# Third product of the attention scores on 64 rows, its two components on different row halves, blocks of scores made in pairs

## The chip, the cores and the metric

The kernel runs on one core of one Trainium2 chip. The metric is the time of one execution on the device, in microseconds. A core has five engines, each with its own queue of instructions that run in order: TensorE (PE; its weight loads are shown apart as PEld), VectorE (DVE), ScalarE (ACT), GpSimd (POOL) and SyncE (SP), which here issues nearly all DMA transfers. Engines wait for each other through semaphores. TensorE multiplies a stationary operand (loaded by a weight load) with a stream of columns, and adds the product up in PSUM.

## What is computed

One decoder layer, x of 2048 tokens by 1024, all in float32: a projection, then two groups of heads side by side (differential attention with 4 heads, and mLSTM with 4 heads), an output projection, and an MLP with squared ReLU. The part that matters is attention. Each head has two components of 64 dimensions, each with its own queries and keys, and one value of 128:

```
s = einsum('bhcqd,bhckd->bhcqk', qb, kb) * scale      # c: 2 components, d: 64
s = where(mask, s, -inf);  p = softmax(s)             # causal
p_diff = p[:, :, 0] - lam * p[:, :, 1]
out = einsum('bhqk,bhkv->bhqv', p_diff, v)            # v: 128
```

## The kernel before

Float32 products are made from two parts. A float32 number x is split into hi (rounded to the type float32r, which TensorE takes in one pass) and lo, the rest. x times y is then hi*hi + hi*lo + lo*hi, three passes (`mm3`, L91 to L95). Some products (transposes, the values of attention, mLSTM) are left in plain float32, of which one product of values or mLSTM shows as two passes in a trace and a transpose as one.

`phase_in` (L189 on) makes the projections, and writes keys and queries of attention, turned and split, to the DRAM tensors Kd and Qd: `Kd[g][h, 0]` is hi and `[h, 1]` is lo, each 128 rows, of which rows 0 to 63 are component 0 and 64 to 127 component 1. `phase_mix` (L503 on) is attention and mLSTM. Its attention goes in 64 units (4 heads h, 16 blocks qb of 128 queries):

- `load_kv` (L528), once in four units: a K tile of 512 keys, [128, 2, 512]. On rows 0 to 63 lies hi and on rows 64 to 127 lo, for component c in `[:, c]`. It takes two DMAs; the values V one.
- `load_q` (L539), once in two units: a Q tile [128, 2, 2, 256]. Both row halves hold the same, hi in `[:, 0]` and lo in `[:, 1]`, per component. Four DMAs.
- `scores` (L549): for each component c and each block j of up to 512 keys two products over all 128 rows into one PSUM tile s (pool psS, three buffers). The first, with Q hi against K hi and lo at once, gives hi*hi + hi*lo; the second, with Q lo, gives lo*hi + lo*lo (L571 to L574). VectorE moves the block from PSUM to the tile p and takes its maximum (L577; the last block with the causal mask, L580). When a component's blocks are done, ScalarE takes exp (L586). After both, p = p0 + cf * p1 is made on VectorE (L596) and, for long rows, in part on ScalarE and GpSimd (L594, L595).
- `values` (L639 on): p is turned by TensorE in 128x128 blocks into tp (L651), copied to pT by ScalarE (L653), and multiplied with V into pv (L656). VectorE writes o (L658).

`ahead` (L614) holds up to four units scored before their values are made. Between the units run the stages of 16 chunks of mLSTM: `chunk_load` (L690; loads E from Md and wb from Wd, each broadcast over rows; GpSimd adds a mask at L705 and ScalarE takes exp at L707), `chunk_scores` (L711; L725 multiplies over 64 rows, the two heads of a pair on different halves), `chunk_values` (L731; L742 over 128 rows and L743 over 64 rows alternate; L749 has 64 columns of the stationary operand) and `chunk_norm`.

The order on each engine is not the order of the code. A scheduler with a timeline of its own sets it when the program is built; each engine then runs its row as it stands.

Of the kernel before, what the change touches and what calls it, by code (L numbers as in the profile page):

```python
# [11 lines left out]
F32 = mybir.dt.float32  # L12
F32R = mybir.dt.float32r
I32 = mybir.dt.int32
AF = mybir.ActivationFunctionType
ALU = mybir.AluOpType
# [486 lines left out]
def phase_mix(tc, a, sc, ident, late):  # L503
    nc = tc.nc
    with ExitStack() as ctx:
        def pool(name, bufs, **kw):
            return ctx.enter_context(tc.tile_pool(name=name, bufs=bufs, reuse_waits="tile", **kw))

        kp = pool("kp", 5, side="right")
        qp = pool("qp", 3, side="right")  # L510
# [3 lines left out]
        psS = pool("psS", 3, space=PSUM)  # L514
        psV = pool("psV", 1, space=PSUM)

        maskq = ce.tile([128, 512], F32, name="maskq")
# [3 lines left out]
        Ks, Vs, Qs, outs = {}, {}, {}, {}  # L521
        n_p = [0]

        def p_tile():
            n_p[0] += 1
            return (pb if n_p[0] % 6 == 0 else pa).tile([128, S], F32, name="p")

        def load_kv(h, g):  # L528
            t = kp.tile([128, 2, 512], F32R, name="K")
            for hl in range(2):  # L530
                nc.sync.dma_start(t[hl * 64:(hl + 1) * 64].bitcast(F32),
                                  sc["Kd"][g][h, hl].rearrange("(c p) t -> p c t", c=2))
            Ks[h, g] = t
            t = kp.tile([128, 4, 128], F32, name="V")
            nc.sync.dma_start(t, sc["Vd"][g][:, h * 128:(h + 1) * 128].rearrange(
                "(b p) v -> p b v", p=128))
            Vs[h, g] = t

        def load_q(h, g):  # L539
            Q = qp.tile([128, 2, 2, 256], F32R, name="Q")  # L540
            o = g % 2 * 256
            for hf in range(2):
                for var in range(2):
                    nc.sync.dma_start(
                        Q[hf * 64:(hf + 1) * 64, var].bitcast(F32),
                        sc["Qd"][g // 2][h, var, :, o:o + 256].rearrange("(c p) t -> p c t", c=2))
            Qs[h, g] = Q

        def scores(u):  # L549
            h, qb = units[u]  # L550
            if qb % 4 == 0:
                load_kv(h, qb // 4)
            if qb % 2 == 0:
                load_q(h, qb // 2)
            Q = Qs[h, qb // 2]
            W = (qb + 1) * 128
            n = qb // 4 + 1
            qo = (qb % 2) * 128
            mx = st.tile([128, 2, 4], F32, name="mx")
            nm = st.tile([128, 2], F32, name="nm")  # L560
            Z = st.tile([128, 2], F32, name="Z")
            if n <= 2:
                t = p_tile()
                p = [t[:, 0:1024], t[:, 1024:2048]]
            else:
                p = [p_tile(), p_tile()]
            for c in range(2):
                pc = p[c]
                for j in range(n):
                    w = min(512, W - j * 512)  # L570
                    ps = psS.tile([128, 512], F32, name="s")  # L571
                    for var in range(2):
                        nc.tensor.matmul(ps[:, :w], Q[:, var, c, qo:qo + 128], Ks[h, j][:, c, 0:w],  # L573
                                         start=(var == 0), stop=(var == 1))  # L574
                    dst = pc[:, j * 512:j * 512 + w]
                    if j < n - 1:
                        nc.vector.tensor_scalar(dst, ps[:, :w], 0.0, None, op0=ALU.add, op1=ALU.max,  # L577
                                                accum_out=mx[:, c, j:j + 1])
                    else:
                        nc.vector.tensor_tensor_reduce(dst, ps[:, :w], maskq[:, 512 - w:512], 1.0, -3.0e38,  # L580
                                                       ALU.add, ALU.max, mx[:, c, j:j + 1])
                if n == 1:
                    nc.vector.tensor_scalar(nm[:, c:c + 1], mx[:, c, 0:1], -1.0, None, op0=ALU.mult)
                else:
                    nc.vector.tensor_reduce(nm[:, c:c + 1], mx[:, c, :n], axis=AX.X, op=ALU.max, negate=True)  # L585
                nc.scalar.activation(pc[:, :W], pc[:, :W], AF.Exp, bias=nm[:, c:c + 1],  # L586
                                     accum_out=Z[:, c:c + 1])
            rz = st.tile([128, 2], F32, name="rz")
            nc.vector.reciprocal(rz, Z)
            cf = st.tile([128, 1], F32, name="cf")  # L590
            nc.vector.scalar_tensor_tensor(cf, Z[:, 0:1], nlam, rz[:, 1:2], op0=ALU.mult, op1=ALU.mult)
            cut = W if W < 1024 else W - int(W * PSH) // 128 * 128
            if cut < W:
                nc.scalar.activation(p[1][:, cut:W], p[1][:, cut:W], AF.Copy, scale=cf)  # L594
                nc.gpsimd.tensor_tensor(p[0][:, cut:W], p[1][:, cut:W], p[0][:, cut:W], op=ALU.add)  # L595
            nc.vector.scalar_tensor_tensor(p[0][:, :cut], p[1][:, :cut], cf, p[0][:, :cut],  # L596
                                           op0=ALU.mult, op1=ALU.add)
            return p[0], rz
# [15 lines left out]
        def ahead(u):  # L614
            held = sum(1 if units[v][1] < 8 else 2 for v in pend)
            while len(pend) < 4:
                v = u + len(pend)
                if v >= len(units):
                    break
                held += 1 if units[v][1] < 8 else 2  # L620
                if held > 7:
                    break
                pend[v] = scores(v)

        pend[0] = scores(0)
        pend[1] = scores(1)
        yield
        raw, w_out = late["raw"], late["w_out"]
# [704 lines left out]
```

## Time and profile before

| | us |
|---|---|
| median of 3 runs (2558.26 to 2561.15) | 2559.36 |
| the profiled execution's own time | 2563.28 |
| its span, first to last instruction | 2561.4 |
| of it 0 to 553.5: projections | 553.5 |
| 553.5 to 1073: attention and mLSTM | 519.5 |
| 1073 to 1281: output projection | 208.0 |
| 1281 to the end: MLP | 1280.4 |

Times in the rows are of one execution. Matmuls are pipelined: the busy time of one includes its way through the array, so a product's own share is read from the distance between starts, not from its length. The granted clock is given as a share of full speed: 1.00 is 2.4 GHz, 0.50 is 1.2 GHz.

### The profile page before, as it was taken

The page shows a single profiled execution, that of the slowest core. Times are in us where ns is not written, and L with a number is a line of the kernel's source. Part 1 is how long each engine was busy: PE and PEld are TensorE (multiplying, and loading weights), DVE is VectorE, ACT ScalarE, POOL GpSimd, SP SyncE. Part 2 cuts the span into 40 slices and gives each one's busy share as a digit, 9 for nine tenths or more (in the row PEclk, how much of TensorE's full clock was granted, in tenths as well). Part 3 has the DMA queues.
Part 4 walks back from the last instruction along what each step waited for, and adds up shares of the span by engine and source line. Part 5 has one row for each costly group of instructions (what it writes and reads, how often), then busy time and mean ns, then how long its engine had stood idle before and what let it go on. Part 6 is the DMA issues. An engine that isn't in the chain of part 4 may idle for free.

```text
span 2561.4 us, 34625 instructions
## 1 busy us (share of the span) xinstructions
PE 2425.0 (95%) x12030; PEld 2040.0 (80%) x12030; DVE 1456.0 (57%) x3132; ACT 1065.2 (42%) x2103; POOL 440.1 (17%) x724
## 2 busy tenths in 40 slices
PE   8999999989879799999939999999999999999998
PEld 6888889987668687888828888888888888887886
DVE  4483441016657588576647667666665543333885
ACT  7210112326656577644524344444444332332433
POOL 0002222104635354432300000000000000000423
PEclk9999999998889899999969999999999999999999
DMA  9323432257653634255774345844358664444784
GB/s 320 130 78 91 125 109 85 55 133 167 145 115 75 148 88 113 83 177 181 236 266 164 136 157 174 350 161 168 133 176 305 222 221 169 146 143 167 282 288 144
DMA packets 296751, 424.35 MB, mean 166 GB/s; under 512 B 23584, under 2 KB 170416, under 8 KB 295040
## 3 DMA queue, kind: packets, MB, share of 16 engines
q1 hardware_dynamic: 296224, 421.94, 51.5%
q8 instruction: 95, 1.56, 0.3%
q14 instruction: 80, 0.66, 0.1%
q0 software_dynamic: 352, 0.20, 0.1%
HBM read 283.56 MB, written 138.49 MB: 165 GB/s over the span
## 4 chain that ended last, share of the span: by engine, by line
PE 76%; DMA 11%; DVE 6%; POOL 2%; ACT 2%; issue 2%; SPq 0%; POOLq 0%; DVEq 0%; ACTq 0%
PE pd L969 16%; PE A L969 14%; PE B L969 10%; PE pp L93 7%; PE pp L94 7%; PE pp L95 7%; DMA br<-in_w_down_dram 3%; PE pv L656 3%; PE s L573 3%; PE po L93 2%; DMA E<-Md 2%; PE po L94 2%; PE po L95 2%; PE tp L651 2%; DMA wb<-Wd 1%
## 5 line engine op out<-in xcount | busy, mean ns | idle before, releaser
L969 PE MATMUL pd<-bo,ao 128*128 128x512 f32 x2688 | 613.8, 390 | 8.3 <-DVE y L1153 4.8
L969 PEld LDWEIGHTS pd<-bo,ao 128*128 128x128 f32 x2688 | 506.2, 188 | 115.8 <-issue 5.2
L969 PE MATMUL A<-B,w 128*128 128x512 f32 x1536 | 359.3, 389 | 0.0
L969 PEld LDWEIGHTS A<-B,w 128*128 128x128 f32 x1536 | 288.3, 188 | 59.7
L969 PE MATMUL B<-B,w 128*128 128x512 f32 x1152 | 274.4, 392 | 19.2 <-ACT w L1059 19.2
L93 PE MATMUL pp<-w,xT 128*128 128x512 f32 (+1 forms) x768 | 271.3, 358 | 9.3 <-ACT w L230 7.8
L94 PE MATMUL pp<-w,xT 128*128 128x512 f32 (+1 forms) x768 | 273.2, 356 | 0.0
L95 PE MATMUL pp<-w,xT 128*128 128x512 f32 (+1 forms) x768 | 271.1, 355 | 0.0
L969 PEld LDWEIGHTS B<-B,w 128*128 128x128 f32 x1152 | 217.9, 189 | 65.0 <-ACT w L1059 19.7
L1211 POOL TENSOR_TENSOR y<-y,g 128x512 f32<-128x512 f32 x32 | 49.2, 1560 | 1183.6 <-ACT jk L1205 1120.2
L1178 ACT CAST ao<-ar 128x1024 fp32r<-128x1024 f32 x112 | 117.8, 1052 | 287.5 <-PE pd L969 150.5
L1153 DVE TENSOR_TENSOR ao<-ar,ao 128x1024 fp32r<-128x1024 f32 x112 | 139.3, 1243 | 152.3 <-ACT ao L1178 152.2
L1026 DVE TENSOR_TENSOR w<-wr,w 128x512 fp32r<-128x512 f32 x224 | 154.0, 689 | 105.0 <-ACT w L1059 103.9
L573 PE MATMUL s<-K,Q 128*128 128x512 f32 (+3 forms) x640 | 193.9, 418 | 13.6 <-DVE p L577 6.6
L1059 ACT CAST w<-wr 128x512 fp32r<-128x512 f32 x224 | 138.8, 621 | 130.6 <-PE B L969 116.8
L656 PE MATMUL pv<-V,pT 128*128 128x128 f32 x1088 | 158.2, 290 | 31.5 <-ACT pT L653 22.9
L656 PEld LDWEIGHTS pv<-V,pT 128*128 128x128 f32 x1088 | 147.4, 202 | 44.0 <-ACT pT L653 26.2
L586 ACT ACTIVATE p<-p,nm 128x128 f32<-128x128 f32 (+15 forms) x128 | 153.5, 1200 | 33.2 <-DVE nm L585 22.1
L93 PEld LDWEIGHTS pp<-w,xT 128*128 128x128 f32 x768 | 144.4, 188 | 25.9 <-ACT w L230 8.7
L577 DVE TENSOR_SCALAR_CACHE_REDUCE p<-s 128x512 f32<-128x512 f32 x192 | 129.0, 684 | 51.6 <-PE s L573 28.4
L94 PEld LDWEIGHTS pp<-w,xT 128*128 128x128 f32 x768 | 144.5, 188 | 15.2 <-DVE w L231 0.3
L95 PEld LDWEIGHTS pp<-w,xT 128*128 128x128 f32 x768 | 144.3, 188 | 15.1
(249 smaller groups left out, 3566.0 us busy)
## 6 DMA issues: line engine op xcount, KB each, us to landing
ud<-u SPq DMA_DIRECT2D x224, 256.0 KB, 2.8
ar<-ud SPq DMA_DIRECT2D x112, 512.0 KB, 4.1
br<-in_w_down_dram SPq DMA_DIRECT2D x224, 256.0 KB, 4.0
wr<-in_w_up_dram SPq DMA_DIRECT2D x128, 256.0 KB, 3.6
Bd<-hl SPq DMA_DIRECT2D x40, 512.0 KB, 3.9
B<-Bd SPq DMA_DIRECT2D x10, 2048.0 KB, 13.8
Q<-Qd SPq DMA_DIRECT2D x128, 128.0 KB, 4.7
raw<-in_xT_dram SPq DMA_DIRECT2D x32, 256.0 KB, 5.0
```

What stands on the lines that cost most here:

```text
L93: nc.tensor.matmul(ps, lhs[0], rhs[0], start=first, stop=False)
L94: nc.tensor.matmul(ps, lhs[0], rhs[1], start=False, stop=False)
L95: nc.tensor.matmul(ps, lhs[1], rhs[0], start=False, stop=last)
L573: nc.tensor.matmul(ps[:, :w], Q[:, var, c, qo:qo + 128], Ks[h, j][:, c, 0:w], start=(var == 0), stop=(var == 1))
L577: nc.vector.tensor_scalar(dst, ps[:, :w], 0.0, None, op0=ALU.add, op1=ALU.max, accum_out=mx[:, c, j:j + 1])
L586: nc.scalar.activation(pc[:, :W], pc[:, :W], AF.Exp, bias=nm[:, c:c + 1], accum_out=Z[:, c:c + 1])
L656: nc.tensor.matmul(pv, pT[:, i * 128:(i + 1) * 128], Vs[h, j][:, i, :], start=(b == 0), stop=(b == nb - 1))
L969: nc.tensor.matmul(ps, l[i], r[j], start=(first and k == 0 and m == 0), stop=(last and k == n - 1 and m == 2), skip_group_check=True)
L1026: self.nc.vector.tensor_tensor(out, x, y, op=op)
L1059: self.nc.scalar.copy(w[:, 0], src)
L1153: nc.vector.tensor_tensor(out, x, y, op=op)
L1178: nc.scalar.copy(l[:, 0], u)
```

## The change

The second product of a block is now made over 64 rows: Q lo against K hi alone. lo*lo is left out. To have it on different rows for the two components, the tiles are laid out anew. In K, component 0 has hi on rows 0 to 63 and lo on 64 to 127, component 1 the other way round; a K tile takes four DMAs of half the size. Q holds hi of both components on both row halves (`[:, 0:2]`) and in `[:, 2]` lo, component 0 on rows 0 to 63 and component 1 on rows 64 to 127; it takes three DMAs. In `scores` the loop over blocks is now outside that over components: for one block, two PSUM tiles are taken, then stand the 128-row products of both components, then both 64-row products, then both evacuations. The exps of both components follow after the last block.

```diff
--- before.py
+++ after.py
@@ -527,9 +527,11 @@
 
         def load_kv(h, g):
             t = kp.tile([128, 2, 512], F32R, name="K")
-            for hl in range(2):
-                nc.sync.dma_start(t[hl * 64:(hl + 1) * 64].bitcast(F32),
-                                  sc["Kd"][g][h, hl].rearrange("(c p) t -> p c t", c=2))
+
+            for c in range(2):
+                for hl in range(2):
+                    r = (hl ^ c) * 64
+                    nc.sync.dma_start(t[r:r + 64, c].bitcast(F32), sc["Kd"][g][h, hl, c * 64:c * 64 + 64])
             Ks[h, g] = t
             t = kp.tile([128, 4, 128], F32, name="V")
             nc.sync.dma_start(t, sc["Vd"][g][:, h * 128:(h + 1) * 128].rearrange(
@@ -537,13 +539,13 @@
             Vs[h, g] = t
 
         def load_q(h, g):
-            Q = qp.tile([128, 2, 2, 256], F32R, name="Q")
+            Q = qp.tile([128, 3, 256], F32R, name="Q")
             o = g % 2 * 256
             for hf in range(2):
-                for var in range(2):
-                    nc.sync.dma_start(
-                        Q[hf * 64:(hf + 1) * 64, var].bitcast(F32),
-                        sc["Qd"][g // 2][h, var, :, o:o + 256].rearrange("(c p) t -> p c t", c=2))
+                nc.sync.dma_start(
+                    Q[hf * 64:(hf + 1) * 64, 0:2].bitcast(F32),
+                    sc["Qd"][g // 2][h, 0, :, o:o + 256].rearrange("(c p) t -> p c t", c=2))
+            nc.sync.dma_start(Q[:, 2].bitcast(F32), sc["Qd"][g // 2][h, 1, :, o:o + 256])
             Qs[h, g] = Q
 
         def scores(u):
@@ -564,21 +566,26 @@
                 p = [t[:, 0:1024], t[:, 1024:2048]]
             else:
                 p = [p_tile(), p_tile()]
+            for j in range(n):
+                w = min(512, W - j * 512)
+                pair = [psS.tile([128, 512], F32, name="s") for _ in range(2)]
+                for c in range(2):
+                    nc.tensor.matmul(pair[c][:, :w], Q[:, c, qo:qo + 128], Ks[h, j][:, c, 0:w],
+                                     start=True, stop=False)
+                for c in range(2):
+                    r = slice(c * 64, c * 64 + 64)
+                    nc.tensor.matmul(pair[c][:, :w], Q[r, 2, qo:qo + 128], Ks[h, j][r, c, 0:w],
+                                     start=False, stop=True)
+                for c in range(2):
+                    dst = p[c][:, j * 512:j * 512 + w]
+                    if j < n - 1:
+                        nc.vector.tensor_scalar(dst, pair[c][:, :w], 0.0, None, op0=ALU.add, op1=ALU.max,
+                                                accum_out=mx[:, c, j:j + 1])
+                    else:
+                        nc.vector.tensor_tensor_reduce(dst, pair[c][:, :w], maskq[:, 512 - w:512], 1.0, -3.0e38,
+                                                       ALU.add, ALU.max, mx[:, c, j:j + 1])
             for c in range(2):
                 pc = p[c]
-                for j in range(n):
-                    w = min(512, W - j * 512)
-                    ps = psS.tile([128, 512], F32, name="s")
-                    for var in range(2):
-                        nc.tensor.matmul(ps[:, :w], Q[:, var, c, qo:qo + 128], Ks[h, j][:, c, 0:w],
-                                         start=(var == 0), stop=(var == 1))
-                    dst = pc[:, j * 512:j * 512 + w]
-                    if j < n - 1:
-                        nc.vector.tensor_scalar(dst, ps[:, :w], 0.0, None, op0=ALU.add, op1=ALU.max,
-                                                accum_out=mx[:, c, j:j + 1])
-                    else:
-                        nc.vector.tensor_tensor_reduce(dst, ps[:, :w], maskq[:, 512 - w:512], 1.0, -3.0e38,
-                                                       ALU.add, ALU.max, mx[:, c, j:j + 1])
                 if n == 1:
                     nc.vector.tensor_scalar(nm[:, c:c + 1], mx[:, c, 0:1], -1.0, None, op0=ALU.mult)
                 else:
```

What the scheduler makes of it on TensorE, at a unit of two blocks (512 and 384 keys) in the third head. Names: s is a PSUM tile of scores, tp a transpose, pv a product with values, m an mLSTM product; "x2" are two in a row. Before:

```order
L743 MATMUL m_9582<-C_4820,wb_9346 128x130
L573 MATMUL s_7974<-K_7476,Q_7965 128x512 x2
L651 MATMUL tp_8013<-ident_211,p_7831 128x128 x4
L573 MATMUL s_7978<-K_7873,Q_7965 128x384 x2
L573 MATMUL s_7984<-K_7476,Q_7965 128x512 x2
L656 MATMUL pv_7912<-V_7479,pT_7916 128x128 x2
L651 MATMUL tp_8107<-ident_211,p_7886 128x128 x4
L573 MATMUL s_7988<-K_7873,Q_7965 128x384 x2
```

After, at the same unit (L573 is the product over 128 rows, L577 that over 64; s_7975 is component 1 of the first block, s_7982 and s_7983 are the pair of the second; lines from here on stand 7 higher than before, so L663 is pv and L749 the mLSTM product that was L742):

```order
L663 MATMUL pv_7913<-V_7481,pT_7917 128x128 x2
L573 MATMUL s_7975<-K_7476,Q_7966 128x512
L577 MATMUL s_7975<-K_7476,Q_7966 128x512
L573 MATMUL s_7982<-K_7873,Q_7966 128x384
L577 MATMUL s_7982<-K_7873,Q_7966 128x384
L573 MATMUL s_7983<-K_7873,Q_7966 128x384
L577 MATMUL s_7983<-K_7873,Q_7966 128x384
L749 MATMUL m_9582<-vaug0_4817,E_9344 128x130
```

The four products of a pair are not in the order of the code: each 64-row product stands right behind its own 128-row product. Of the 320 products of L577, 309 stand alone so; four times two and once three stand in a row. Where a row of TensorE goes from products of 128 rows and columns to others (64 rows, or 64 columns of the stationary operand) or back, its shape changes: 210 times in the program before, 803 times in the one after.

On SP, whose row issues the DMAs, the loads of keys, values and queries for the second group of 512 keys. Before:

```order
L544 DMA Q<-Qd_67 64x2x256 x2
L531 DMA K<-Kd_64 64x2x512 x2
L535 DMA V<-Vd_72 128x4x128
L544 DMA Q<-Qd_68 64x2x256 x6
L393 DMA mvd<-t_4758 128x344
```

After:

```order
L545 DMA Q<-Qd_67 64x2x256
L548 DMA Q<-Qd_67 128x256
L534 DMA K<-Kd_64 64x512 x4
L537 DMA V<-Vd_72 128x4x128
L545 DMA Q<-Qd_68 64x2x256 x2
L548 DMA Q<-Qd_68 128x256
```

K has four issues of half the size; a Q tile has two issues of 64 rows and one of 128 in place of four. The number of issues for K and Q stays at 160.

## Rows read from the trace of the kernel before

**Rows 1.** The page: busy time of the engines, granted clock in 40 slices

```profile
PE 2425.0 (95%) x12030; PEld 2040.0 (80%) x12030; DVE 1456.0 (57%) x3132; ACT 1065.2 (42%) x2103; POOL 440.1 (17%) x724
PEclk9999999998889899999969999999999999999999
```

**Rows 2.** Busy us by stretch, the stage of attention and mLSTM

```profile
core 0: us, PE busy (x) PEld busy (x) DVE busy (x) ACT busy (x) POOL busy (x), PEclk, DMA share, GB/s
553.50:1073.00 519.50, 449.93 (x2851) 378.95 (x2852) 355.23 (x1247) 332.87 (x808) 241.60 (x556) 0.91 0.51 121
```

**Rows 3.** Chain of waits in that stage, its shares by line

```profile
by line: PE pv L656 14.7%; PE s L573 13.6%; DMA E<-Md 10.7%; PE tp L651 7.6%; DMA wb<-Wd 5.6%; DMA Q<-Qd 3.5%; ACT p L586 3.5%; DVE p L577 3.3%; PE m L743 3.2%; issue 3.1%; PE m L742 3.0%; POOL E L705 2.3%; DVE p L580 2.1%; DVE p L596 2.1%;
```

**Rows 4.** A group in that stage: busy us, mean ns, idle before

```profile
L573 PE MATMUL s<-K,Q 128*128 128x512 f32 x448 | 154.6, 449 | 10.2 <-DVE p L577 5.4 <-DMA Q<-Qd 3.5 <-DVE mx L580 0.9
```

**Rows 5.** The same view, VectorE's evacuation of a block

```profile
L577 DVE TENSOR_SCALAR_CACHE_REDUCE p<-s 128x512 f32<-128x512 f32 x192 | 129.0, 684 | 51.6 <-PE s L573 28.4 <-PE tp L651 12.3 <-POOL p L595 9.3
```

**Rows 6.** Busy us by stretch, a stretch of the last matrix product

```profile
2000.00:2100.00 100.00, 100.00 (x443) 82.84 (x442) 54.70 (x70) 32.47 (x45) 0.00 (x0) 1.00 0.70 232
```

**Rows 7.** TensorE in order of time: start us, us, operation, count

```profile
938.16 0.71 PE L651 MATMUL tp<-ident,p 128*128 128x128 f32 x5
938.80 0.72 PE L725 MATMUL m<-qk 64*128 64x128 f32 x8
939.45 1.55 PE L573 MATMUL s<-K,Q 128*128 128x512 f32 x6
941.15 0.49 PE L743 MATMUL m<-C,wb 64*128 64x130 f32 x2
941.57 0.49 PE L742 MATMUL m<-vaug,E 128*128 128x130 f32 x2
```

**Rows 8.** The same view, scores ahead of a 64-row product

```profile
675.16 0.71 PE L573 MATMUL s<-K,Q 128*128 128x512 f32 x2
675.80 0.71 PE L725 MATMUL m<-qk 64*128 64x128 f32 x4
676.44 0.50 PE L573 MATMUL s<-K,Q 128*128 128x512 f32 x1
```

**Rows 9.** TensorE's waits in the stage: total us, times, longest

```profile
PE pv L656 <- ACT pT L653: 22.9, 8, 4.8
PE tp L651 <- ACT pT L653: 17.2, 4, 6.9
PE tp L651 <- DVE p L596: 0.7, 2, 0.4
```

**Rows 10.** One wait for E, all engines in order of time

```profile
749.30 0.37 SPq L699 DMA_DIRECT2D E<-Md  x1
750.26 1.63 PE L573 MATMUL s<-K,Q 128*128 128x512 f32 x6
755.70 1.88 PE L573 MATMUL s<-K,Q 128*128 128x128 f32 x8
759.08 1.26 POOL L705 TENSOR_TENSOR E<-E,masks 128x512 f32<-128x512 f32 x1 [9.09 <-DMA E<-Md]
760.38 1.28 ACT L707 ACTIVATE E<-E,aS 128x128 f32<-128x128 f32 x4 [7.24 <-POOL E L705]
764.44 0.90 PE L651 MATMUL tp<-ident,p 128*128 128x128 f32 x3 [6.86 <-ACT pT L653]
```

**Rows 11.** TensorE in order of time while the clock was low

```profile
870.66 0.80 PE L743 MATMUL m<-C,wb 64*128 64x130 f32 x2
871.39 0.80 PE L742 MATMUL m<-vaug,E 128*128 128x130 f32 x2
872.91 0.27 PE L651 MATMUL tp<-ident,p 128*128 128x128 f32 x1
```

**Rows 12.** Busy us by stretch, an idle piece and the stage's start

```profile
759.80:763.20 3.40, 0.00 (x0) 0.00 (x0) 0.00 (x0) 2.82 (x7) 2.94 (x9) 0.50 0.13 27
560.00:600.00 40.00, 30.57 (x160) 24.35 (x159) 26.39 (x103) 20.31 (x53) 8.75 (x7) 0.82 0.94 186
```


## Prediction

> **What bounds the kernel now.** I read the page first. TensorE is busy for 95% of the span [rows 1], so nearly everything is a matter of TensorE; but the line of its granted clock dips in slices 9 to 16, and that is where attention and mLSTM run. The busy time by stretch gives that stage as 553.5 to 1073: 519.5 us, in which TensorE is busy 450 us, VectorE 355, ScalarE 333 and GpSimd 242, at a mean granted clock of 0.91 [rows 2]. The edit lies in this stage alone, and the order of the program differs only there. The chain of waits of that stage is not TensorE's alone: the lines pv, s, tp and m of TensorE hold 42% of it, the loads E, wb and Q 20%, the rest is ScalarE, VectorE and GpSimd in turn [rows 3]. So work added to TensorE is paid in part and swallowed in part, and the prediction is about how much. Among TensorE's groups the score products (s) come second, 448 of the widest form [rows 4].
>
> **The columns that the change saves: nothing.** Each block of scores had two products over 128 rows; now the second runs over 64 rows. A product streams its columns whatever its rows are: two 64-row passes of L743 take 0.49 us, and so do two 128-row passes of L742 beside them, of 130 columns both [rows 7]. A gain needs the two 64-row products of a pair side by side, on the two halves of the array. That this works is to be seen: eight 64-row passes of L725, on the two halves in turn, take from 938.80 to 939.45, 0.65 us [rows 7], where four of one half and one line take 0.64 (675.80 to 676.44) [rows 8]. The Trainium skill (TensorEngine Tiling (Array Packing), Tiling Modes) has the same, that different tiles load weights and multiply in parallel; by it alone the change would take away the time of every second 64-row product. What that is: the 64-row products have 139,264 columns, half of them 69,632, or 136 times 512. The stream of 512-column products elsewhere runs at 443 in 100 us, 0.226 us each [rows 6], so 31 us. But the order of the changed program does not set the two beside each other. Of 320 such products 309 stand alone between other products, as the order rows on the change show; the rest are four twos and one three, which save 1 us at most. I take 0.
>
> **The changes of shape that it adds: 119 us of TensorE's time.** In the rows of mLSTM 128-row and 64-row products alternate, and their groups of two passes start at 941.15 and 941.57, 0.42 us apart, and so on for eight groups [rows 7]. Passes of one shape follow each other faster: five of tp take 0.71 us, a single one 0.27 [rows 7, 11], so (0.71 - 0.27) / 4 = 0.11 each and 0.22 for two. One change of shape costs 0.42 - 0.22 = 0.20 us. The weight loads tell why: between equal shapes they lie under the running product (82.8 us of loads inside 100 us full of products [rows 6]); at a change the load begins only when the product ahead is through. The score products pay it too: two of them take 0.64 us ahead of L725 (675.16 to 675.80) [rows 8] where two of the stream take 0.45, 0.19 more. Counted in the order, TensorE's row changes shape 210 times before and 803 times after: 593 more, at 0.20 us 119 us at the full clock. No row shows a 512-column product of 64 rows, so bounds: 0.19 (113 us) and 0.20 (119 us) per change; below that there is no row. I take 119.
>
> **What waits swallow: 40 us.** In the stage TensorE's waits sum to 69 us in the listing of who waited for whom, eleven rows from 22.9 to 0.7; the two largest, 22.9 and 17.2 us, are on pT of ScalarE [rows 9]. One of them in full [rows 10]: the load of E is issued at 749.30, just behind the last m products; GpSimd starts on it at 759.08 (it had waited 9.09), ScalarE's E at 760.38 had waited 7.24 with the copy of pT queued behind it, and TensorE's tp starts at 764.44 after 6.86. All that time depends on the load. Between 749.5 and 757.6 TensorE had 8 us of work, fourteen score products among it in two rows alone [rows 10]; a change of shape more for each makes it 2.8 us longer and this wait 40% shorter. With the other score products and the smaller gaps that no row of waits counts I take a little over half of 69 us: 40 us. Ends: 15 us, if the waits move to other places with the new order, and 69, all of it.
>
> **The clock: +60 us.** After such a wait the granted clock is at the lower of its two levels, 1.2 GHz: 759.80 to 763.20 at 0.50 with TensorE idle [rows 12]. Now the gaps at each change of shape are added, in every block of scores, and at the lower clock they grow: the same group of m takes 0.73 us from 870.66 to 871.39 [rows 11], against 0.42. So I expect the clock to fall more often and to come back later. The nearest row for a stage with more emptiness is its first 40 us, which had 0.82 [rows 12]; I take 0.80 for the whole. At 0.91 of 519.5 us some 93 us were at the lower level; at 0.80 of about 640 us it is 256 us, 163 more. A microsecond there costs at most half, and 0.42 of 0.73 us by the m group; as some of these stretches are waits anyway I take 0.37: 60 us. Ends: 0, if the mean clock stays, and 135, at a mean of 0.70 over 720 us (432 us, 339 more, at 0.40).
>
> **The rest: 0.** The blocks are made pair by pair, so both exps of a unit come behind its last pair, where the first used to run under the second component's scores. One exp has 1.2 us on the page; up to four units are scored ahead, which covers it. Without that cover it is 64 times 1.2 = 77 us; I leave 15 us of it in the upper end. Three PSUM buffers for pairs of two could make TensorE wait for VectorE, whose evacuation takes 0.68 us a block [rows 5]; but a block now occupies TensorE for 2 x 0.42 = 0.85 us, no longer 0.45, so VectorE keeps up. K comes in four loads instead of two, Q in three instead of four: 160 issues on SP's queue before and after, 4 MB less in all; it delays nothing.
>
> **Sum.** 119 - 40 + 60 = 139 us on the profiled execution's 2563.3 us (span 2561.4 and 1.9 around it): 2702. The median of the runs is 3.9 us lower, so I predict 2698.
>
> **The rivals.** *The clock holds.* If the mean stays at 0.91 and waits swallow 55 us, 119 - 55 = 64: 2623. For it: with fewer long waits there are fewer falls. Against it: every block of scores has gaps now. Chance 0.26. *The clock stays low.* Once at the lower level, with score blocks that are half gaps, it may not come back for long; at 0.70 the sum is 119 - 40 + 135 = 214: 2773, and 2800 with the exps' 15 and little swallowed. For it: the m groups at the lower clock, 0.73. Against it: runs of pv and tp without a gap lie between. Chance 0.11. *Not slower: the loads set the stage's length.* If the time from the last m products over the load of E to the next pT decides each of the 16 chunks, TensorE's 119 us have to fit under it. Then nothing of the 119 is paid: 2559. It decides only from a cover of 119 us on, and the waits give 69. Chance 0.03. *Faster: the halves do run side by side,* and changes of shape cost nothing for these products: 2559 - 31 = 2528. The order of the program speaks against the first, the 0.64 us of [rows 8] against the second. The Trainium skill (TensorE: Matmul & The Clock Gate, Part 3) would have it so in one respect: there a weight load passes under running products only if its rows differ. The rows here say the contrary, loads of equal rows are covered. Chance 0.02.
>
> **How the numbers follow.** The forecast has 0.58, with 2640 to 2760 as its own range; 0.26 lies at 2605 to 2640, 0.11 at 2760 to 2840, 0.05 at 2559 or less. A range of 2605 to 2800 leaves out 0.05 below and some 0.07 above, and takes in the ends of the unknown terms: 119 - 69 = 50 (2609) and 119 - 15 + 135 = 239 (2798). A measurement of this kernel tells 0.2% from no change. Faster by more than that: 0.02; within it: 0.03; slower: 0.95.
>
> **What would show it.** In the changed profile: the s groups of L573 and L577 starting 0.42 us apart at full clock, not 0.23; a stage of 640 to 670 us where 519.5 stood; a mean granted clock near 0.80 in it; fewer waits on pT; the time outside the stage unchanged within 2 us. The prediction is wrong if 64-row and 128-row products of s follow each other at 0.23 us, if pairs of L577 start together in the trace, or if the stage's clock stays above 0.88.

## The result, and the profile after

The changed kernel takes 2638.2 us (median of four runs, 2627.4 to 2653.8) against 2559.4 us before: a ratio of 1.031, with an interval of 1.026 to 1.037. It is slower by 79 us. The four runs differ by more than those of before; their mean granted clocks are 0.969, 0.967, 0.964 and 0.958, in the order of their times. The profiled execution is the fastest of them, 2627.41 us with a span of 2625.5, so the traces differ by 64 us and the medians by 79.

The page of after (busy time, share of the span, instructions; then the granted clock in 40 slices), beside [rows 1]:

```profile
PE 2539.1 (97%) x12030; PEld 2055.5 (78%) x12030; DVE 1462.6 (56%) x3132; ACT 1070.5 (41%) x2103; POOL 437.3 (17%) x724
PEclk9999999988979899999988999999999999999999
```

TensorE has the same 12030 instructions and is busy for 114 us more; its weight loads (PEld) take 15 us more, and no other engine moved by more than 7. The clock dips in the same part of the span. The busy time by stretch: the stage of attention and mLSTM, its first 40 us, and 20 us full of score products (busy us and instructions per engine, granted clock, DMA share, GB/s):

```profile
553.50:1142.00 588.50, 564.36 (x2857) 393.89 (x2855) 363.19 (x1247) 338.42 (x810) 239.34 (x556) 0.91 0.37 101
560.00:600.00 40.00, 37.67 (x116) 23.57 (x114) 20.72 (x78) 16.98 (x46) 8.10 (x7) 0.62 0.58 156
1042.00:1062.00 20.00, 19.94 (x97) 12.95 (x97) 17.31 (x64) 13.73 (x32) 12.27 (x45) 1.00 0.16 50
```

Against [rows 2] the stage is 69 us longer (588.5 for 519.5). TensorE is busy for 114.4 us more in it and idle for 45.4 us less (24.1 for 69.6): 114.4 - 45.4 = 69, the whole growth. The mean clock of the stage is 0.91, as before, although its first 40 us have 0.62 where [rows 12] had 0.82. With the ends that the table below uses, from the last product of the projections to the first of the output projection, the stage grew by 68 us (582.2 for 514.2) and TensorE's busy time in it by 113; what lies outside became 4 us shorter.

TensorE's row in a place full of score products at the full clock (start, duration, line), where the products of 128 rows (L573) and of 64 (L577) alternate:

```profile
1042.04 0.49 PE L577 MATMUL s<-K,Q 64*128 64x512 f32 x1
1042.46 0.50 PE L573 MATMUL s<-K,Q 128*128 128x512 f32 x1
1042.89 0.50 PE L577 MATMUL s<-K,Q 64*128 64x512 f32 x1
1043.32 0.49 PE L573 MATMUL s<-K,Q 128*128 128x512 f32 x1
```

And the same at the lower clock:

```profile
765.69 0.79 PE L577 MATMUL s<-K,Q 64*128 64x512 f32 x1
766.41 0.79 PE L573 MATMUL s<-K,Q 128*128 128x512 f32 x1
767.13 0.79 PE L577 MATMUL s<-K,Q 64*128 64x512 f32 x1
```

The starts are 0.43 us apart at the full clock and 0.72 at the lower, not 0.226 as in a stream of products of one shape. The groups of the stage (busy us, mean ns | idle before), beside [rows 4]:

```profile
L577 PE MATMUL s<-K,Q 64*128 64x512 f32 x224 | 114.6, 518 | 0.0
L573 PE MATMUL s<-K,Q 128*128 128x512 f32 x224 | 114.6, 514 | 2.2 <-DVE p L582 1.2 <-DVE mx L585 1.0
```

The same 448 products were 154.6 us of busy time; now they are 229.2. Every second one now has half the rows and is no shorter for it. Last, the chain of waits in the stage, and TensorE's waits there (us, times, longest), beside [rows 3] and [rows 9]:

```profile
by line: PE pv L663 22.4%; PE s L577 18.3%; PE s L573 14.9%; PE tp L658 10.9%; DMA od<-mog 4.4%; PE m L749 4.4%; PE m L750 4.4%; DMA E<-Md 3.2%; PE m L732 2.2%; PE m L756 1.8%; DMA mog<-mod 1.7%; issue 1.4%; PE m L723 1.1%; ACT p L593 0.9%;
...
PE pv L663 <- ACT pT L660: 6.7, 3, 3.7
PE m L756 <- ACT ns L751: 5.1, 2, 4.2
PE s L573 <- DVE mx L585: 3.1, 4, 1.6
...
PE tp L658 <- ACT pT L660: 1.9, 2, 1.6
```

TensorE's lines hold 80% of the chain where they held 42%, and of the loads of E, wb and Q, which had 20%, only E is among the rows, with 3.2%. The two large waits on pT, 22.9 and 17.2 us before, are 6.7 and 1.9; all of TensorE's waits together went from 69 to 24 us.

### The profile page after: what moved, and what is told of

It reads as the page before. It is cut to its first block, busy times and chain, and to the rows that moved or that the text cites. A ratio compares the mean times of both kernels' runs of the same rounds, so it can differ in the third digit from the quotient of the medians.

```text
span 2625.5 us, 34606 instructions
## 1 busy us (share of the span) xinstructions
PE 2539.1 (97%) x12030; PEld 2055.5 (78%) x12030; DVE 1462.6 (56%) x3132; ACT 1070.5 (41%) x2103; POOL 437.3 (17%) x724
## 4 chain that ended last, share of the span: by engine, by line
PE 84%; DMA 8%; DVE 4%; ACT 1%; issue 1%; POOL 1%; SPq 0%; POOLq 0%; DVEq 0%; ACTq 0%
PE pd L976 15%; PE A L976 13%; PE B L976 10%; PE pp L93 6%; PE pp L94 6%; PE pp L95 6%; PE pv L663 5%; PE s L577 4%; PE s L573 3%; DMA br<-in_w_down_dram 3%; PE tp L658 2%; PE po L93 2%; PE po L95 2%; PE po L94 2%; DMA Bd<-hl 1%
## 5 line engine op out<-in xcount | busy, mean ns | idle before, releaser
L663 PE MATMUL pv<-V,pT 128*128 128x128 f32 x1088 | 168.2, 302 | 8.2 <-ACT pT L660 6.7
L663 PEld LDWEIGHTS pv<-V,pT 128*128 128x128 f32 x1088 | 146.6, 209 | 27.6 <-issue 9.5
L573 PE MATMUL s<-K,Q 128*128 128x512 f32 (+3 forms) x320 | 151.6, 477 | 4.3 <-DVE mx L585 3.1
```

Source lines behind the costliest of these rows:

```text
L573: nc.tensor.matmul(pair[c][:, :w], Q[:, c, qo:qo + 128], Ks[h, j][:, c, 0:w], start=True, stop=False)
L663: nc.tensor.matmul(pv, pT[:, i * 128:(i + 1) * 128], Vs[h, j][:, i, :], start=(b == 0), stop=(b == nb - 1))
```

## The experiments

Theory: a change of shape in TensorE's row costs TensorE 0.2 us, waits swallow a part, and nothing else in the change matters. Rivals: the order (pairs, later exps, halved loads of K) costs the time; the clock does; and, once the waits are used up, each further change is paid in full. All kernels are compared with the kernel before on the same chip. The table has, of each, the changes of shape in TensorE's row as its order has them, the difference of the medians, and from its profiled execution the length of the stage (here from the last product of the projections to the first of the output projection), TensorE's busy time and the sum of its waits in it, the time at the lower clock with the number of stretches, and how much of that time TensorE was busy. Only this last part can make TensorE's work longer.

| kernel | changes | against before, us | ratio, interval | stage, us | TensorE busy, us | waits, us | lower clock, us (stretches) | of it busy, us |
|---|---|---|---|---|---|---|---|---|
| before | 210 | | | 514.2 | 444.7 | 69 | 89 (15) | 70 |
| after | 803 | +79 | 1.0312 [1.0258, 1.0366] | 582.2 | 558.1 | 24 | 109 (11) | 104 |
| e1_pairs_128rows | 219 | +17 | 1.0053 [1.0035, 1.0072] | 528.8 | 459.4 | 68 | 106 (14) | 87 |
| e2_64rows_alone | 809 | +75 | 1.0295 [1.0257, 1.0332] | 582.1 | 557.4 | 25 | 116 (10) | 106 |
| e3_one_component | 504 | +35 | 1.0127 [1.0105, 1.0149] | 544.9 | 500.5 | 44 | 106 (10) | 95 |
| e4_adjacent | 521 | +49 | 1.0177 [1.0150, 1.0203] | 562.2 | 496.5 | 65 | 133 (16) | 116 |
| e7_adjacent_four | 501 | +17 | 1.0067 [1.0049, 1.0084] | 534.4 | 471.9 | 62 | 96 (12) | 82 |
| e8_one_m | 228 | +16 | 1.0057 [1.0037, 1.0078] | 526.9 | 452.2 | 76 | 102 (15) | 76 |
| e5_padded | 82 | -3 | 0.9993 [0.9980, 1.0005] | 509.6 | 422.8 | 87 | 82 (13) | 61 |
| e6_adjacent_padded | 398 | +30 | 1.0120 [1.0106, 1.0133] | 546.9 | 467.4 | 78 | 116 (18) | 96 |
| e12_after_padded | 682 | +64 | 1.0252 [1.0230, 1.0273] | 572.1 | 533.1 | 39 | 102 (14) | 97 |
| e9_late_E | 213 | +6 | 1.0016 [1.0002, 1.0029] | 519.7 | 455.9 | 64 | 99 (13) | 89 |
| e10_after_late_E | 805 | +67 | 1.0270 [1.0246, 1.0294] | 579.6 | 566.0 | 13 | 126 (10) | 123 |
| e11_padded_late_E | 86 | -11 | 0.9965 [0.9952, 0.9978] | 504.4 | 419.2 | 85 | 75 (14) | 58 |

### The order without the 64 rows

The pairs and K's layout of after, but the second product over 128 rows and Q as before:

```diff
-  r = slice(c * 64, c * 64 + 64)
-  nc.tensor.matmul(pair[c][:, :w], Q[r, 2, qo:qo + 128], Ks[h, j][r, c, 0:w],
+  nc.tensor.matmul(pair[c][:, :w], Q[:, 1, c, qo:qo + 128], Ks[h, j][:, c, 0:w],
```

> The changed kernel with its pairs, its four loads of K and its late exps, but the third product over all 128 rows again (Q lo on both halves, as before). TensorE's row changes shape 219 times, where before has 210 and the changed kernel 803. If the changes of shape cost the time: 2559 us, give or take 12 for another order. If the pairs, the two PSUM tiles taken at once or the exps behind the last pair cost it: near 2638.

Measured +17 us, more than the 12 that I had allowed for another order, with waits as before (68 us). TensorE's busy time is 15 us longer; 17 us more of it lie at the lower clock (87 for 70), which is worth some 7 us at the 0.42 worked out below. What the other 8 us are no run shows. The order by itself has a small price; most of the 79 us is not in it.

### The 64 rows without the order

The kernel before, with its second product on rows 0 to 63 for both components, which leaves out the same lo*lo as the change does:

```diff
+  r = slice(0, 128 if var == 0 else 64)
-  nc.tensor.matmul(ps[:, :w], Q[:, var, c, qo:qo + 128], Ks[h, j][:, c, 0:w],
+  nc.tensor.matmul(ps[:, :w], Q[r, var, c, qo:qo + 128], Ks[h, j][r, c, 0:w],
```

> The kernel before, component after component, with its own loads; only the second product of a block runs over 64 rows (both components on rows 0 to 63). 809 changes of shape. If the changes of shape cost the time: 2620 to 2655, as the changed kernel. If the pairs and the layout cost it: 2559.

Measured +75 us, the same stage, the same waits, the same count of changes as after. So the 64 rows alone are enough to cause it; which half they lie on, and the pairing, add nothing on top that these intervals can tell. The two differences are known to 10 and 14 us, so e1's 17 us could still hide between them.

### Half the dose

Only component 0 on 64 rows (`64 if c == 0 else 128`):

> As the run with 64 rows alone, but for component 0 only: 504 changes of shape, 294 more than before, 56 us of TensorE at 0.19 each. If waits swallow the first part of what is added (TensorE's waits sum to 69 us before, 24 in the changed kernel): less than half of the 79 us that the full dose cost, 2570 to 2590. If nothing is swallowed and the cost is in proportion: 2599. If the granted clock carries much of it: also above 2599.

Measured +35 us for 294 more changes, 47% of e2's 75 us for 49% of its changes: 0.12 us for each in the first half of the dose, 0.13 in the second. TensorE's busy time grows by 56 and 57 us, and the waits fall from 69 to 44 to 25, by 25 and 20 us. So waits don't swallow the first changes whole and then run out; they take some 40% of what is added in either half.

### The halves side by side

The change as its words have it: an order edge sets both 64-row products of a pair behind both 128-row ones, so that all 160 pairs stand together in TensorE's row.

```diff
-  nc.tensor.matmul(pair[c][:, :w], Q[r, 2, qo:qo + 128], Ks[h, j][r, c, 0:w],
-                   start=False, stop=True)
+  half = nc.tensor.matmul(pair[c][:, :w], Q[r, 2, qo:qo + 128], Ks[h, j][r, c, 0:w],
+                          start=False, stop=True)
+  behind(half, full[1])
```

> The changed kernel with one more order given to the scheduler: both 64-row products of a pair behind both 128-row products, so all 160 pairs stand side by side on TensorE. 521 changes of shape, 311 more than before: 59 us at 0.19. If the two halves run side by side, 31 us come off, 28 us are left on TensorE and half of that in the time: 2565 to 2585. If they don't: 2590 to 2605. If the changes of shape cost nothing and side by side is what counts: 2528.

Measured +49 us (2604.6), more than the 2565 to 2585 that I had expected if the halves run side by side. TensorE's row (L577 is here the 128-row product, L581 that over 64):

```profile
902.60 0.48 PE L577 MATMUL s<-K,Q 128*128 128x512 f32 x1
903.01 0.49 PE L581 MATMUL s<-K,Q 64*128 64x512 f32 x2
903.43 0.50 PE L577 MATMUL s<-K,Q 128*128 128x512 f32 x1
```

Two 64-row products of 512 columns go in 0.42 us together, no longer than one of them alone (0.43 in after). The halves do run side by side. But 0.42 is also 0.2 more than one product takes in a stream, so a pair gives back one product (0.226) and still pays its changes of shape. And a new wait is there (us, times, longest):

```profile
PE s L577 <- DVE p L587: 14.5, 25, 3.4
PE s L577 <- DVE mx L590: 10.9, 11, 5.4
```

The score products now wait for VectorE to empty their PSUM tiles: 25 us, where after has 4 (3.1 on mx above, and 1.2 on p). TensorE's busy time in the stage is 62 us below after's (496.5 for 558.1), and its waits are 41 us longer (65 for 24), 21 of them in these two rows. The clock has a part too: e4 has the most time at the lower level of all kernels, 133 us, and TensorE is busy in 116 of it, where before has 70; those 46 us more are worth some 19 of the 49 us at 0.42 each.

### A fourth tile for the scores

To take that wait away e7 gives the scores a fourth PSUM tile, out of the two of mLSTM; e8 is before with that one mLSTM tile.

```diff
-  psM = pool("psM", 2, space=PSUM)
+  psM = pool("psM", 1, space=PSUM)
+  psX.append(pool("psX", 1, space=PSUM))
```

> The adjacent pairs with four PSUM tiles for scores instead of three; the fourth is taken from the two of mLSTM. If the 25 us of TensorE's waits on VectorE's evacuation, which the adjacent pairs brought, come from pairs of two in three tiles: they go, and the time falls to 2580 to 2592. If they come from the late maximum and exps, or the lost mLSTM tile costs as much: 2600 to 2610.

> The kernel before with one PSUM tile for mLSTM instead of two: what the tile that the four-tile run takes away costs by itself. 2557 to 2575; mLSTM has 16 chunks with seven such tiles each, and a wait of some 0.1 us per tile would be 11 us.

e7 takes +17 us against e4's +49. The waits of the scores on VectorE fall from 25.4 to 16.6 us in all, as these rows of e7 have it, but others on pT grow:

```profile
PE tp L672 <- ACT pT L674: 23.2, 6, 5.5
PE pv L677 <- ACT pT L674: 13.9, 8, 3.7
PE s L585 <- DVE p L595: 8.6, 5, 5.9
PE s L585 <- DVE mx L598: 8.0, 3, 7.4
```

So the gain is not the wait that the tile was to remove: the sum of the waits is 62 us for 65, and what fell is TensorE's busy time, by 25 us, of which some 15 us would be the clock (82 us busy at the lower level for 116, at 0.42). Whether the fourth tile brought that about no run shows.

e8 is +16 us, the price of the lost mLSTM tile. So beside e8, which has the same one tile, adjacent pairs cost 1.5 us: the 273 changes of shape more (501 for 228, 55 us of TensorE at 0.2) and the time of 157 products less (31 us by the prediction's count) come out even within what the runs can tell. Even then the change gains nothing.

### Fewer changes of shape in mLSTM

If a change costs 0.2 us anywhere, taking some away must give it back. L743 multiplies over 64 rows between products of 128; with zeros in the other half of its stationary operand it can run over all 128:

```diff
-  nc.tensor.matmul(o, qw[hp:hp + 64, r, :], C[hp:hp + 64, r, :], start=False, stop=True)
+  nc.tensor.matmul(o, qw[:, e2, r, :], C[:, r, :], start=False, stop=True)
```

> The kernel before, with no 64-row product beside the 128-row ones in the values of mLSTM: the rows of Wd and q are kept in tiles whose other half is zero, so L743's product runs over 128 rows and gives the same sum. GpSimd multiplies twice over 64 rows instead of once over 128. TensorE's row changes shape 82 times instead of 210. If each change costs 0.19 to 0.20 us of TensorE and some 60% of it comes through, as in the three runs so far: 128 x 0.2 x 0.6 = 15 us less, 2540. If these changes lie under the waits for E: 2555. If the new steps of GpSimd or the late loads of wb cost more: above 2560.

> The adjacent pairs together with the padded mLSTM product: 398 changes of shape instead of 521. By the same account 15 us below the adjacent pairs alone: 2590. If the waits on VectorE for PSUM tiles set the adjacent pairs' time: 2600 to 2605.

> The changed kernel with the padded mLSTM product: 682 changes of shape instead of 803. In the kernel before, the same edit took 128 changes away and gave nothing, as TensorE's waits grew by 18 us. In the changed kernel TensorE waits for 24 us only. If what counts is how near TensorE is to being the bound: the 121 changes at 0.19 to 0.20, 23 us, come through for the most part, 15 to 23 us below the changed kernel, 2615 to 2624 where it has 2638. If a change is worth 0.13 us anywhere: 16 below. If the padded product gives nothing in itself: 2638.

In e5, before with this edit, the time stays (0.9993), where I had expected 15 us less. TensorE's busy time in the stage fell by 22 us (428.6 for 450.4 from 553.5 to the first product of the output projection), 0.17 us for each of 128 changes:

```profile
553.50:1069.50 516.00, 428.59 (x2864) 370.46 (x2865) 359.52 (x1249) 333.24 (x810) 252.44 (x574) 0.92 0.52 124
...
PE pv L656 <- ACT pT L653: 32.6, 12, 6.5
PE tp L651 <- ACT pT L653: 16.3, 3, 6.2
```

but its waits grew from 69 to 87. Here TensorE alone doesn't decide. In the other two the same edit gave time back: e6 is +30 where e4 was +49, 19 us for 123 changes, and e12 +64 where after was +79, 15 us for 121 changes (0.15 and 0.12 us each; both steps lie between runs on different chips). Their busy time fell by 29 and 25 us, and their waits grew by 14 and 15.

### Is it the load of E that makes the waits?

The prediction had read one long wait as the load of E (GpSimd's mask and ScalarE's exps on it stand in front of the copies of pT). e9 orders those instructions behind the normalization of the chunk before:

```diff
+  if c:
+      later(add, last["pool"])
+      for e in exps:
+          later(e, last["act"])
```

> The kernel before, with one order more: the mask and the exps of E of a chunk stand behind the normalization of the chunk before on GpSimd's and ScalarE's rows; its loads stay as early as before. If the copies of pT wait because E's exps stand too early in ScalarE's row, ahead of a load that takes 10 us: the 40 us of TensorE's waits on pT mostly go, and the time falls by 15 to 30 us, 2530 to 2545. If the waits come from elsewhere, or the later exps hold up mLSTM's scores: 2560 or more.

> The changed kernel with the same order more. If the waits for E are what swallows a part of the changes of shape: with them gone before and after, the change costs more than the 75 to 79 us that it costs with them, 85 to 105 above the kernel before with late E; 2620 to 2640. If the waits swallow nothing and the price is simply 0.13 us per change: again 75 to 79 above it.

> The padded mLSTM product, 86 changes of shape, with the same order more. The padded product alone gave nothing: TensorE's waits grew from 69 to 87 us in its profile. If they grew because the waits for E stood behind: now some 15 to 25 us below the kernel before with late E, 2510 to 2530. If not: equal to it within 5 us.

e9 missed: +6 us, where a gain was expected. The waits on pT halve, but their sum hardly moves (64 for 69), because others stand in their place, as these rows of e9 show beside [rows 9]:

```profile
PE pv L656 <- ACT pT L653: 10.2, 6, 4.5
PE s L573 <- DVE p L577: 9.1, 10, 3.2
PE tp L651 <- ACT pT L653: 9.0, 2, 4.9
PE s L573 <- DMA Q<-Qd: 8.2, 3, 4.4
PE m L753 <- DVE E L738: 6.0, 3, 3.4
PE tp L651 <- POOL p L595: 5.9, 2, 5.7
```

e10, the change on top of it, is 61 us above e9, and swallows as much as on before: 51 us of waits (64 to 13), though pT's waits on E had been halved. I had expected 85 to 105. So how much is swallowed doesn't hang on those waits. In e11 the padded product on top of e9 gives 17 us (2550 for 2567), 0.13 us for each of 127 changes. Not all of it is the changes: TensorE's busy time fell by 37 us, but it is busy at the lower clock for 31 us less (58 for 89), which is worth some 13 of the 37; the waits grew by 21. It is 11 us faster than the kernel before, 0.9965 [0.9952, 0.9978]: a small gain, but it beats both kernels, with fewer changes of shape, not with more.

## Why the prediction was right, and where a term was off

I predicted 2698 us in 2605 to 2800. The direction and the mechanism, changes of shape in TensorE's row, are right. That 2638 lies in the range is owed in part to its width: it is just below the 2640 to 2760 that I had given the forecast itself, and inside the 2605 to 2640 of the rival "the clock holds", which had a chance of 0.26. The rival's sum, 64 us, is that of the two traces, but by luck: its terms, 119 and 55, are not the measured ones.

**Columns saved: 0. Right.** In after nearly all these products stand alone and their rows start 0.43 us apart. e4 shows that the rival's condition, pairs together, would have saved a product's time per pair, and that the changes of shape would still be there: the rival "faster" fails on its second condition as well as on its first.

**Changes of shape: +119. Right in kind, some 20 us too large.** The busy time of TensorE in the stage grew by 113 us, the clock's part of some 14 in it (below). That leaves about 99 us for 593 changes, 0.17 each, though 0.43 - 0.226 = 0.20 us stands in the rows where the shapes alternate. Why the sum over the stage comes to less no run shows. The row that I took 0.19 from was misread: in this stage two score products take 0.56 us, not 0.45, also ahead of a product of their own shape,

```profile
784.39 0.72 PE L573 MATMUL s<-K,Q 128*128 128x512 f32 x2
784.95 0.38 PE L656 MATMUL pv<-V,pT 128*128 128x128 f32 x2
```

so the 0.64 of [rows 8] shows 0.08 us of a change, not 0.19. e2 pins the cost on the 64 rows. The Trainium skill (TensorEngine Tiling (Array Packing), Key Properties) says that a change of the tiling mode drains TensorE; the rows agree, at 0.20 us for each change. The weight loads of after, in the same place as the first rows above, show where that time goes:

```profile
1042.04 0.18 PEld L577 LDWEIGHTS s<-K,Q 64*128 64x128 f32 x1 [0.24 <-issue]
1042.46 0.19 PEld L573 LDWEIGHTS s<-K,Q 128*128 128x128 f32 x1 [0.24 <-DVE nm L592]
```

Each load begins only with its own product, 0.42 us after the product ahead began, and lasts 0.18 or 0.19 us; between products of one shape it lies under the one ahead. So most of the 0.20 us is a load that nothing covers. No run varied the load and the change of shape separately.

**Waits swallow 40. Right in size (45), wrong in cause.** I had laid it on the load of E. With E's mask and exps moved back (e9, e10) 51 us were swallowed. And e3 shows much the same share in either half of the dose (25 of 56 us, then 20 of 57), not a store that is used up first. My reading is that wherever TensorE takes longer, the other engines get ahead of it by as much, and any wait that follows is shorter; that is argued from the sums, not shown for single waits.

**The clock: +60. This is the step that failed.** I took the mean of the stage to fall to 0.80; it stayed at 0.91. By one of my own signs the prediction is wrong in this ("if the stage's clock stays above 0.88"), and the sign "a stage of 640 to 670 us" failed with it (588). The trace of after has 109 us at the lower level in the stage, before had 89. What counts is when TensorE works there: 104 us of the 109, and 70 of the 89. These 34 us more cost 0.42 each (0.30 of 0.72 in the score rows), an estimate of some 14 us. My nearest row was the first 40 us of the stage, and that stretch did get worse, 0.82 to 0.62. But I spread it over the whole stage.

The mechanism that I feared is there in part. In before each of the 15 falls comes within a few us of an idle piece of TensorE. In after eight of the 11 do, as here (a product of values that had waited 3.66 us; the score product behind it runs at 0.77 us where 0.49 is the full clock's):

```profile
863.46 1.16 PE L663 MATMUL pv<-V,pT 128*128 128x128 f32 x8 [3.66 <-ACT pT L660]
...
864.59 0.77 PE L573 MATMUL s<-K,Q 128*128 128x512 f32 x1
```

The other three, at 612.0, 844.1 and 1011.4, come while TensorE is at work without a pause by its record, in which the 0.2 us of a change of shape don't show as idle time. The last of them (columns as above; the clock is the third number from the end):

```profile
1004.60:1011.40 6.80, 6.80 (x27) 3.93 (x26) 5.33 (x22) 6.80 (x19) 1.19 (x1) 1.00 0.52 165
1011.40:1014.80 3.40, 3.40 (x17) 3.40 (x17) 0.44 (x3) 3.39 (x11) 0.00 (x0) 0.50 0.67 217
```

Such falls stand in the traces of e2 (four of 10), e10 (five of 10) and e12 (four of 14) too, all with 682 changes or more, and in none of the kernels with 521 or fewer. This speaks for the alternation bringing the clock down with no wait, though no run isolates it and it need not come so: 1042 to 1062 above keeps 1.00. Once down, the clock also came back later: two stretches at the lower level are 30.7 and 23.9 us long in after, where before had none over 14. Against this, waits became fewer and with them the falls that follow a wait, eight for 15, and so the sum rose by no more than 20 us. The other three runs of after, at means of 0.967 to 0.958, are 7 to 26 us longer than the profiled one; by the mean clock the slowest has some 58 us more at the lower level (0.011 x 2 x 2640), worth 24 us at 0.42. In those runs the clock took more of my 60; they have no trace, so this is worked out only.

**The rest: 0. Open.** Where the order stands alone it costs 17 us (e1). On top of the 64 rows it costs nothing that shows: after has it, e2 doesn't, and the 4 us between them are well within the intervals. Outside the stage 4 us were gained, not 2.

**The sum again,** with what the traces show: TensorE's busy time grew by 113 us, some 99 for the changes and 14 for the clock; less 45 of waits this is 68 in the stage, less 4 outside it 64, the difference of the profiled executions. My sum was 139. The clock makes 46 of the 75 us between the two, the changes 20, the waits 5 and the time outside 4.

**Open.** Why before alone returns nothing for the 128 changes that e5 takes away, while the same edit returns 15 to 19 us in e6, e11 and e12: in e5 the waits grew by 18 us where the busy time fell by 22, in the other three by 14 to 21 where it fell by 25 to 37, and no run says why they took more there. The e6 and e12 steps go across chips, e11's does not.

## What to carry to other kernels

Fewer rows in a product save nothing by themselves, and each change between shapes in TensorE's row costs 0.2 us there, of which 0.12 us reached the time in a stage where TensorE was 87% busy when changes were added to it, and nothing when some were taken away (e5). A row of half-height products has to stand together, in the order that the engine really runs, in runs long enough to pay for two changes; count the changes in the order before building, and see that the PSUM tiles suffice for the pairs. Sums of waits move as a whole: taking one cause away (E here) brought up the next, so the largest row among the waits is not what its removal gives. And time at the lower clock has to be counted where the engine works: e7 gained more over e4 through it, some 15 us, than through the waits that its edit was meant to remove.

## What was unexpected of the hardware

The clock can stay at its lower level for long with TensorE never out of work for long. Two stretches of after (columns as above), and the busy share in them is 98%:

```profile
567.60:598.30 30.70, 30.07 (x90) 19.85 (x90) 14.36 (x47) 11.19 (x26) 8.10 (x7) 0.50 0.57 146
755.40:779.30 23.90, 23.55 (x67) 15.35 (x67) 11.21 (x35) 11.17 (x31) 7.64 (x19) 0.50 0.35 70
```

Both are full of products that alternate in shape, score products above all. At the full clock the same alternation kept 1.00 for 20 us in one place (1042 to 1062), and in three others the clock fell in the midst of it without a wait. Also, a change of shape costs more at the lower clock, but not in proportion to everything: a product with its change takes 0.72 us there against 0.43, a factor of 1.7, not 2.
